# Diffusion trunk on one core: squares summed on DVE, second halves of five tiles, and two output tiles summed in one round

## Chip, cores and metric

The kernel runs on one core of a Trainium2 chip. The metric is device time in microseconds (us) of one execution. Engines: TensorE (PE), VectorE (DVE), ScalarE (ACT), GpSimd (POOL); SyncE (SP) issues the weight loads.

## The reference

One inference step of a two-layer trunk over 128 context tokens and 512 latent tokens (640 columns here), width 1024, all in fp32. Cut to what matters:

```python
for i in range(DEPTH):                       # 2 layers
    mod = (silu(cond) @ ada_w[i] + ada_b[i]) # 9 vectors of 1024: shifts, scales, gates
    h = modulate(rms_norm(x, norm_g[i, 0]), mod[:, 0], mod[:, 1])
    x = x + 0.5 * mod[:, 2] * swiglu(h, ffn_w_in[i, 0], ffn_w_out[i, 0])
    h = modulate(rms_norm(x, norm_g[i, 1]), mod[:, 3], mod[:, 4])
    o = even_mixer(h, ...) if i % 2 == 0 else odd_mixer(h, ...)   # both end in "@ w_out"
    x = x + mod[:, 5] * o
    h = modulate(rms_norm(x, norm_g[i, 2]), mod[:, 6], mod[:, 7])
    x = x + 0.5 * mod[:, 8] * swiglu(h, ffn_w_in[i, 1], ffn_w_out[i, 1])
y = rms_norm(x, final_norm)
```

The even mixer joins retention heads and spatial gating groups, the odd one is differential attention. Each of the six steps of the two layers is a phase here, 0 to 5; number 6 is the final norm.

## The kernel before

**Tiles.** Activations lie with channels on partitions and tokens along the free axis, in eight blocks of 128 channels. Tokens go in two halves, hf=0 and hf=1, of 320 columns each. An fp32 product is the sum of three matmuls (`mm3`, L717 to L719): high part by high part, low part of the activation by the high part of the weight, high part by the low part of the weight.

**Weights.** SP loads blocks of up to 1 MB into `raw` buffers, two at a time. A splitter makes pieces of them: the high part `whi` on ACT (L326), the remainder `wlo` on DVE (L327). There are five buffers for either part, and a piece is held until its last matmul is done. Loads of the adaLN weights `ada_w` go the same way; `ada` multiplies them with silu(cond) on TensorE (`adaps`, L469), copies the result out of PSUM (`adac`, on ACT at L477 or on DVE at L479), and sums the partial rows with L482.

**Projections back to x.** `out_proj` serves the second FFN matrix and the even mixer's output; each of its column groups gi (0 to 3) has two tiles j=0, 1. `op_step` sums a tile (gi, j, hf) in PSUM and `x_update` (L835, on DVE) adds it to x. The first two groups are done for both halves; then come the groups 2 and 3 for hf=0, then for hf=1. The last chunk of weights therefore stays until hf=1 has used it.

**Norm chains.** As soon as x of hf=0 is complete, `norm_chain` runs beside the tiles of hf=1. Squares are formed on ACT (L546) and summed on DVE (L550). TensorE sums over partitions (n10p for phase 1, L565; n20p, ... for the others). DVE works out one over the root in small steps (n10m, n10h, n10y, n10a, n10o, n10e, n10r) and builds diagonals n10d (L574), and TensorE spreads the result over all partitions (n10b, L577). H1t, H1h, H1l and the like (L629, L631, L636) are the next phase's normalised input in high and low parts. How many `mm3` steps pass in front of n10p and of n10b is set by the tables `NW` and `NB`. In these stretches TensorE's order is written by hand; that of DVE and ACT comes from a scheduler, in which chain and weight pieces share one queue.

**The head.** At the start eight blocks of x are squared on ACT (L1565). DVE adds the first `NQ` of them (L1571), and TensorE sums the rest together with DVE's sum (n0p, L1578), five columns of 128 tokens for each operand. While that goes on, `first_wide` runs the `ada` rounds of the first two modulation vectors (letters a and b of the table `SQ`) between the first matmuls `pf` of phase 0. Here the order of PE, DVE and ACT is that of the code.

**The odd mixer's output.** Its weight has two chunks of four heads, c=0 and c=1. The sums over c=0 (tiles m = 4 gp + 2 gi + j) are done during attention, in between the heads, and added to x; those of c=1 follow, hf=0 and then hf=1. The last head's transposes in attention are aot7a and aot7b (L1042).

## Time and profile before

| | us |
|---|---|
| median of 3 runs (lowest to highest) | 2433.4 (2432.97 to 2436.87) |
| profiled execution | 2431.29 |
| its span | 2429.5 |
| TensorE busy | 2389.4 (98%) |
| DVE busy | 1776.3 (73%) |
| ACT busy | 1063.9 (44%) |

The mean granted clock of TensorE is 0.994 of full. The chain that ended last is TensorE for 91% of the span, DVE for 4%, ACT and DMA for 2% each. An idle time of TensorE is therefore paid in full unless something else is late too; one of the other engines costs nothing by itself.

### The profile page before, as it was taken

How to read it: one execution, taken by the hardware profiler on the slowest of the kernel's cores; microseconds unless marked ns; L12 is line 12 of the kernel's file. 1: busy time of each engine (PE TensorE's matmuls, PEld its weight loads, DVE VectorE, ACT ScalarE, POOL GpSimd, SP SyncE). 2: the span in 40 equal slices, each digit the busy share in tenths (PEclk: the TensorE clock that was granted, in tenths of full speed). 3: DMA queues.
4: the chain of work that ended last, by engine and by line, in shares of the span. 5: the costliest groups of instructions: out<-in, count | busy, mean ns of one | idle time of the engine just before them, and what ended most of it. 6: DMA issues, size and time to landing. Idle time of an engine off the chain costs nothing.

```text
span 2429.5 us, 41107 instructions
## 1 busy us (share of the span) xinstructions
PE 2389.4 (98%) x16770; PEld 2338.1 (96%) x16770; DVE 1776.3 (73%) x3652; ACT 1063.9 (44%) x2013; POOL 54.0 (2%) x82
## 2 busy tenths in 40 slices
PE   8999999999999999999999999999999999999998
PEld 6999999999999999999999999999999989999997
DVE  5677767677968777676777776778789888574664
ACT  4425334333326344253543524446776645252442
POOL 0000000000000000000000000001011000000000
PEclk8999999999999999999999999999999999999999
DMA  6342413333242323333323242322111122222121
GB/s 238 148 147 88 156 70 113 129 136 123 90 157 87 139 90 122 129 113 139 122 79 141 98 153 104 122 106 76 44 43 59 55 105 86 72 87 87 70 105 44
DMA packets 44477, 259.33 MB, mean 107 GB/s; under 512 B 5888, under 2 KB 8576, under 8 KB 16768
## 3 DMA queue, kind: packets, MB, share of 16 engines
q1 hardware_dynamic: 41024, 252.37, 28.9%
q8 instruction: 131, 2.15, 0.3%
q0 software_dynamic: 1280, 2.62, 0.3%
q10 hardware_dynamic: 1984, 1.72, 0.2%
q14 instruction: 58, 0.48, 0.1%
HBM read 252.76 MB, written 3.93 MB: 106 GB/s over the span
## 4 chain that ended last, share of the span: by engine, by line
PE 91%; DVE 4%; ACT 2%; DMA 2%; issue 1%; POOL 0%; POOLq 0%; ACTq 0%; DVEq 0%
PE op L718 9%; PE op L717 9%; PE op L719 9%; PE pu L717 7%; PE pu L719 7%; PE pu L718 7%; PE pf L717 4%; PE pf L719 4%; PE pf L718 4%; PE pg L719 4%; PE pg L718 4%; PE pg L717 4%; PE oq L717 1%; PE atb L1422 1%; PE oq L718 1%; DVE wlo L327 1%
## 5 line engine op out<-in xcount | busy, mean ns | idle before, releaser
L327 DVE TENSOR_TENSOR wlo<-raw,whi 128x1024 fp32r<-128x1024 f32 (+1 forms) x482 | 531.6, 1119 | 277.5 <-ACT whi L326 275.6
L326 ACT ACTIVATE whi<-raw 128x1024 fp32r<-128x1024 f32 (+2 forms) x481 | 462.8, 977 | 601.1 <-PE op L718 146.9
L835 DVE SCALAR_TENSOR_TENSOR xs<-op,mod,xs 128x128 f32<-128x128 f32 (+2 forms) x312 | 124.1, 434 | 134.9 <-PE op L719 134.5
L546 ACT ACTIVATE nq<-xs 128x320 f32<-128x320 f32 x84 | 38.7, 467 | 116.1 <-DVE xs L835 114.6
L717 PE MATMUL oq<-H4h,whi 128*128 128x320 f32 x256 | 81.1, 318 | 0.2 <-ACT ov L1034 0.2
L719 PE MATMUL oq<-H4h,wlo 128*128 128x320 f32 x256 | 79.6, 311 | 0.0
L718 PE MATMUL oq<-H4l,whi 128*128 128x320 f32 x256 | 79.3, 310 | 0.0
L1371 DVE TENSOR_REDUCE amx<-as 128x1 f32<-128x320 f32 x144 | 61.5, 459 | 19.2 <-PE as L1367 18.8
L428 DVE CUSTOM_DVE_ANT_0 raw<-raw,sb 128x1024 f32<-128x1024 f32 x60 | 72.9, 1220 | 0.7
L1379 ACT ACTIVATE ap<-as,anm 128x320 f32<-128x320 f32 x128 | 66.1, 530 | 14.1 <-DVE anm L1374 13.7
L717 PE MATMUL pf<-H0p,whi 128*128 128x320 f32 x200 | 63.0, 317 | 0.0
L719 PE MATMUL pf<-H0p,wlo 128*128 128x320 f32 x200 | 62.3, 312 | 0.5 <-DVE wlo L327 0.5
L718 PE MATMUL pf<-H0p,whi 128*128 128x320 f32 x200 | 62.0, 311 | 0.0
L426 DVE SCALAR_TENSOR_TENSOR raw<-raw,sb 128x1024 f32<-128x1024 f32 x48 | 58.3, 1220 | 0.5
L924 ACT COPY p<-pg 128x320 f32<-128x320 f32 x75 | 32.0, 427 | 51.6 <-PE pg L719 51.6
L718 PE MATMUL pf<-H2p,whi 128*128 128x320 f32 x172 | 53.1, 309 | 0.0
L718 PE MATMUL pf<-H5p,whi 128*128 128x320 f32 x172 | 53.1, 309 | 0.0
L307 DVE TENSOR_TENSOR raw<-raw 128x512 f32<-128x512 f32 x75 | 51.7, 689 | 1.9
L718 PE MATMUL pf<-H3p,whi 128*128 128x320 f32 x172 | 53.1, 309 | 0.0
L717 PE MATMUL pf<-H2p,whi 128*128 128x320 f32 x172 | 53.0, 312 | 0.0
L717 PE MATMUL pf<-H5p,whi 128*128 128x320 f32 x172 | 53.0, 312 | 0.0
L717 PE MATMUL pf<-H3p,whi 128*128 128x320 f32 x172 | 53.0, 312 | 0.0
(2686 smaller groups left out, 8769.6 us busy)
## 6 DMA issues: line engine op xcount, KB each, us to landing
raw<-in_w_fin SPq DMA_DIRECT2D x88, 1024.0 KB, 4.8
raw<-in_ada_w SPq DMA_DIRECT2D x64, 1024.0 KB, 4.8
raw<-in_w_fout SPq DMA_DIRECT2D x32, 1024.0 KB, 4.7
raw<-in_w_fout SPq DMA_DIRECT2D x16, 768.0 KB, 4.1
raw<-in_w_oin SPq DMA_DIRECT2D x12, 1024.0 KB, 4.8
raw<-in_w_ein SPq DMA_DIRECT2D x10, 1024.0 KB, 4.8
raw<-in_ada_w SPq DMA_DIRECT2D x32, 256.0 KB, 6.5
raw<-in_w_eout SPq DMA_DIRECT2D x4, 1024.0 KB, 4.7
```

The costliest lines, as they stand in the source:

```text
L307: sub.tensor_tensor(out=a11, in0=a22, in1=a11, op=ALU.subtract)
L326: S.activation(out=hf, in_=t, func=AF.Copy)
L327: sub.tensor_tensor(out=lf, in0=t, in1=hf.bitcast(F32), op=ALU.subtract)
L426: V.scalar_tensor_tensor(out=o, in0=w, scalar=1.0, in1=sb[:, c * D:(c + 1) * D], op0=ALU.mult, op1=ALU.mult, accum_out=r)
L428: V.tensor_tensor_reduce(out=o, in0=w, in1=sb[:, c * D:(c + 1) * D], scale=1.0, scalar=0.0, op0=ALU.mult, op1=ALU.add, accum_out=r)
L546: S.activation(out=q[:, :n], in_=x[k][:, t0:t1], func=AF.Square)
L717: PE.matmul(o, wh, xh, start=start, stop=False, skip_group_check=more)
L718: PE.matmul(o, wh, xl, start=False, stop=False, skip_group_check=more)
L719: PE.matmul(o, wl, xh, start=False, stop=stop, skip_group_check=more)
L835: V.scalar_tensor_tensor(out=x[m][:, a:b], in0=ps[:, a - t0:b - t0], scalar=mod[:, l, gmod * KD + m, c:c + 1], in1=x[m][:, a:b], op0=ALU.m ...
L1371: V.tensor_reduce(out=mx[:, j, a:a + 1], in_=sps[j][a][:, 0:w], axis=AX.X, op=ALU.max, negate=True)
L1379: S.activation(out=pj[j][:, a * 320:a * 320 + w], in_=sps[j][a][:, 0:w], func=AF.Exp, bias=b, accum_out=(sm[:, j, a:a + 1] if full else s2 ...
```

## The change

Three parts. In the head `NQ` is 8, so DVE adds all squares, and the `ada` rounds of `first_wide` are given ACT for their copies. In `out_proj` the first part ends after three tiles of the first two groups (cut=3), and tile (1, 1) is done for hf=1 in the second half, which has five tiles in place of four; for the weight blocks in `jkeys` a piece now holds one output column block j over all k, so that half a block can be given back. The end (nxt=6) keeps its four tiles. In the odd mixer the c=0 sums of the two tiles gp=1, gi=1 of hf=1 are left out of attention; the weight piece is held, and in hf=1 those two tiles sum c=0 and c=1 in one PSUM round of 24 matmuls, ahead of the others. `NP5` and `NB5` place n50p and n50b.

```diff
-NQ = 5
+NQ = 8
 NB = (9, 9)
+NP5 = 11
+NB5 = 16
...
+    jkeys = {("fout", l, s, 2, g) for l, s in ((0, 0), (0, 1), (1, 0)) for g in (1, 2, 3)} | {("eout", g) for g in (1, 2, 3)}
...
+        elif key in jkeys:
+            nq, n = 1, wtab[key][1] * P
+            t = r[:, :2 * n].rearrange("p (k m x) -> p m k x", m=2, x=P)[:, h]
...
+            if order[self.j] in jkeys:
+                return [v[:, k * P:(k + 1) * P] for v in self.piece(m)]
...
-        yield NB[hf] if i < len(PHASES) else 9
+        yield (NB5 if (i, hf) == (5, 0) else NB[hf]) if i < len(PHASES) else 9
...
-                gs.append(ada(order[st["i"]]))
+                gs.append(ada(order[st["i"]], S))
...
     def out_proj(keys, acts, l, gmod, nxt, ks=None):
-        nw = len(keys) if nxt is None else 2
-        for gi in range(nw):
-            W = next_group(keys[gi])
+        end = nxt == len(PHASES)
+        js = [(gi, j) for gi in range(4) for j in range(2)]
+        cut = len(js) if nxt is None else 4 if end else 3
+        Ws = {}
+        for gi, j in js[:cut]:
+            if j == 0:
+                Ws[gi] = next_group(keys[gi])
...
+            for hf in range(2):
+                op_step(keys[gi], Ws[gi], gi, j, hf, acts, l, gmod, nxt, ks)
+                mid_ada()
+            if keys[gi] in jkeys:
+                Ws[gi].drop(j)
+            elif j == 1:
+                Ws[gi].done()
...
-            for gi in (2, 3):
-                if n_ == 0:
+            for gi, j in js[cut:]:
+                if gi not in Ws:
                     Ws[gi] = next_group(keys[gi])
...
-        def oo_step(c, gp, gi, j, hf, W, ps=None):
+        def oo_step(c, gp, gi, j, hf, W, ps=None, W0=None):
             m = 4 * gp + 2 * gi + j
-            for k in range(0 if ps is None else 3, 4):
+            if W0 is not None:
+                ps = psm(f"oo2{m}{hf}")
+                for k in range(4):
+                    mm3(ps, W0, j, 4 * gi + k, acts[k], hf, k == 0, False)
+            for k in range(3 if ps is not None and W0 is None else 0, 4):
...
-                    for hf in range(2):
+                    for hf in range(2 - gp * gi):
                         oo_step(0, gp, gi, j, hf, W)
-            W.done()
+            W.drop(*range(2 - gp))
+        held = W
...
-            for gp in range(2):
-                for gi in range(2):
-                    for j in range(2):
-                        oo_step(1, gp, gi, j, hf, Ws[gp], pss.get((gi, j)) if (hf, gp) == (0, 0) else None)
+            for gp, gi in ((0, 0), (0, 1), (1, 0), (1, 1)) if hf == 0 else ((1, 1), (0, 0), (0, 1), (1, 0)):
+                for j in range(2):
+                    oo_step(1, gp, gi, j, hf, Ws[gp], pss.get((gi, j)) if (hf, gp) == (0, 0) else None,
+                            held if hf * gp * gi else None)
```

How instructions move, at three places. First, ACT's order in the head from the last H0p of the first k row on. Before:

```order
L631 ACTIVATE H0p_148<-H0t_163,mod 128x320
L631 ACTIVATE H0p_149<-H0t_163,mod 128x192
L631 ACTIVATE H0p_149<-H0t_163,mod 128x128
L631 ACTIVATE H0p_150<-H0t_164,mod 128x320
L631 ACTIVATE H0p_151<-H0t_164,mod 128x192
L631 ACTIVATE H0p_151<-H0t_164,mod 128x128
L604 ACTIVATE H0t_164<-H0t_164,mod 128x512
```

After:

```order
L641 ACTIVATE H0p_148<-H0t_163,mod 128x320
L641 ACTIVATE H0p_149<-H0t_163,mod 128x192
L641 ACTIVATE H0p_149<-H0t_163,mod 128x128
L487 COPY adac_5_341<-adaps_5_332 128x256
L487 COPY adac_1_358<-adaps_1_349 128x256
L641 ACTIVATE H0p_150<-H0t_164,mod 128x320
L641 ACTIVATE H0p_151<-H0t_164,mod 128x192
```

The two copies, which stood on DVE, now stand between two H0p groups on ACT. Second, DVE at the boundary to phase 1, from the end of the small steps n10a to the diagonals n10d; `wlo` is a remainder of weights. Before:

```order
L509 SCALAR_TENSOR_TENSOR n10a_4774<-n10o,n10h 128x1 x3
L327 TENSOR_TENSOR wlo_1_4820<-raw_4705,whi_1_4819 128x1024
L520 SCALAR_TENSOR_TENSOR n10e<-n10a_4774 128x1 x3
L835 SCALAR_TENSOR_TENSOR xs<-op_0_2_2_11_4770,mod,xs 128x192
L835 SCALAR_TENSOR_TENSOR xs<-op_0_2_2_11_4770,mod,xs 128x128
L524 SCALAR_TENSOR_TENSOR n10r<-n10e,n10o 128x1
L327 TENSOR_TENSOR wlo_0_4838<-raw_4715,whi_0_4837 128x1024
L524 SCALAR_TENSOR_TENSOR n10r<-n10e,n10o 128x1 x2
L574 TENSOR_SCALAR n10d<-cst,n10r 128x128
L550 TENSOR_TENSOR nq_4418<-nq_4418,nq_4812 128x320
L574 TENSOR_SCALAR n10d<-cst,n10r 128x128
L574 TENSOR_SCALAR n10d<-cst,n10r 128x64
```

After:

```order
L335 TENSOR_TENSOR wlo_0_4729<-raw_4663,whi_0_4728 128x1024
L519 SCALAR_TENSOR_TENSOR n10a_4711<-n10y,n10h 128x1 x3
L560 TENSOR_TENSOR nq_4406<-nq_4406,nq_4721 128x320
L534 SCALAR_TENSOR_TENSOR n10o<-n10a_4711,n10y 128x1 x3
L519 SCALAR_TENSOR_TENSOR n10a_4732<-n10o,n10h 128x1 x3
L530 SCALAR_TENSOR_TENSOR n10e<-n10a_4732 128x1 x3
L534 SCALAR_TENSOR_TENSOR n10r<-n10e,n10o 128x1 x2
L845 SCALAR_TENSOR_TENSOR xs<-op_0_2_2_01_4724,mod,xs 128x192
L534 SCALAR_TENSOR_TENSOR n10r<-n10e,n10o 128x1
L584 TENSOR_SCALAR n10d<-cst,n10r 128x128 x2
L845 SCALAR_TENSOR_TENSOR xs<-op_0_2_2_01_4724,mod,xs 128x128
L584 TENSOR_SCALAR n10d<-cst,n10r 128x64
```

Two of the three remainders in the chain have moved behind n10d. Third, DVE at the boundary to phase 5, from the last diagonal n50d to the first low part of phase 5's input (H5p). Before:

```order
L574 TENSOR_SCALAR n50d<-cst,n50r 128x64
L550 TENSOR_TENSOR nq_21114<-nq_21114,nq_21183 128x320
L550 TENSOR_TENSOR nq_21114<-nq_21114,nq_21201 128x320
L550 TENSOR_TENSOR nq_21114<-nq_21114,nq_21225 128x320
L629 SCALAR_TENSOR_TENSOR H5t_21254<-xs,coefA,n50b 128x320
L629 SCALAR_TENSOR_TENSOR H5t_21255<-xs,coefA,n50b 128x320
L636 SCALAR_TENSOR_TENSOR H5p_21238<-H5t_21254,mod,H5p_21238 128x320
```

After:

```order
L584 TENSOR_SCALAR n50d<-cst,n50r 128x64
L845 SCALAR_TENSOR_TENSOR xs<-oo_21214,mod,xs 128x192
L845 SCALAR_TENSOR_TENSOR xs<-oo_21214,mod,xs 128x128
L560 TENSOR_TENSOR nq_21080<-nq_21080,nq_21165 128x320
L335 TENSOR_TENSOR wlo_1_21237<-raw_21051,whi_1_21236 128x1024
L639 SCALAR_TENSOR_TENSOR H5t_21260<-xs,coefA,n50b 128x320
L560 TENSOR_TENSOR nq_21080<-nq_21080,nq_21189 128x320
L845 SCALAR_TENSOR_TENSOR xs<-oo_21232,mod,xs 128x192
L845 SCALAR_TENSOR_TENSOR xs<-oo_21232,mod,xs 128x128
L639 SCALAR_TENSOR_TENSOR H5t_21261<-xs,coefA,n50b 128x320
L560 TENSOR_TENSOR nq_21080<-nq_21080,nq_21211 128x320
L646 SCALAR_TENSOR_TENSOR H5p_21244<-H5t_21260,mod,H5p_21244 128x320
```

A remainder and two updates of x (two instructions each) have come in between; three sums of squares stand there in both.

## Rows read from the trace of the kernel before

**Rows 1.** Waits of TensorE, whole span: line, releaser, total us, times, longest.

```profile
PE adaps L482 <- DVE adac L479: 3.3, 2, 2.2
...
PE n20b L577 <- DVE n20d L574: 2.0, 1, 2.0
```

**Rows 2.** Timeline of TensorE, head: start, us, instruction, count [idle before <-releaser].

```profile
16.05 5.77 PE L1578 MATMUL n0p<-cst,nq 128*128 128x1 f32 x40
21.75 1.93 PE L469 MATMUL adaps<-raw,sc 128*32 128x256 f32 x16
...
26.35 1.24 PE L1598 MATMUL n0b<-n0d,cst 128*128 128x320 f32 x4
...
28.41 1.07 PE L469 MATMUL adaps<-raw,sc 128*32 128x256 f32 x16
...
34.58 0.77 PE L482 MATMUL adaps<-cst,adac 128*128 128x128 f32 x4 [1.17 <-DVE adac L479]
...
37.03 1.93 PE L469 MATMUL adaps<-raw,sc 128*32 128x256 f32 x32
...
43.08 1.11 PE L482 MATMUL adaps<-cst,adac 128*128 128x128 f32 x4 [2.17 <-DVE adac L479]
```

**Rows 3.** Stretches: length, busy PE, PEld, DVE, ACT, POOL (count), PEclk, DMA share, GB/s.

```profile
15.60:19.20 3.60, 3.60 (x34) 3.60 (x33) 0.00 (x0) 0.00 (x0) 0.00 (x0) 0.97 0.92 342
19.20:21.80 2.60, 2.60 (x17) 2.58 (x20) 0.00 (x0) 0.00 (x0) 0.00 (x0) 0.50 1.01 335
...
43.00:46.20 3.20, 3.12 (x13) 3.08 (x14) 2.61 (x11) 1.04 (x3) 0.00 (x0) 0.50 0.89 289
484.00:490.00 6.00, 6.00 (x43) 6.00 (x42) 5.92 (x14) 3.25 (x6) 0.00 (x0) 1.00 0.31 94
```

**Rows 4.** Timeline of DVE and then of ACT, head, the same columns.

```profile
8.66 3.62 DVE L1571 TENSOR_TENSOR nq<-nq,nq 128x640 f32<-128x640 f32 x4 [7.19 <-ACT nq L1565]
...
23.95 1.07 DVE L1595 TENSOR_SCALAR n0d<-cst,n0r 128x128 f32<-128x128 f32 x5
...
23.75 0.37 ACT L477 COPY adac<-adaps 128x256 f32<-128x256 f32 x1 [8.73 <-PE adaps L469]
...
32.45 1.20 ACT L631 ACTIVATE H0p<-H0t,mod 128x320 fp32r<-128x320 f32 x3 [0.92 <-DVE H0t L629]
...
40.93 1.00 ACT L604 ACTIVATE H0t<-H0t,mod 128x512 f32<-128x512 f32 x2
```

**Rows 5.** SP's issue of the load, and its median us to landing, 25.9 to 26.5.

```profile
26.10 0.33 SPq L264 DMA_DIRECT2D raw<-in_ada_w  x1
...
raw<-in_ada_w SPq DMA_DIRECT2D x1, 256.0 KB, 5.3
```

**Rows 6.** Timelines of TensorE, ACT and DVE, boundary to phase 1, by start.

```profile
466.72 1.93 PE L469 MATMUL adaps<-raw,sc 128*32 128x256 f32 x32
...
472.72 1.06 ACT L326 ACTIVATE whi<-raw 128x1024 fp32r<-128x1024 f32 x1 [4.84 <-DMA raw<-in_w_ein]
...
473.81 1.23 DVE L327 TENSOR_TENSOR wlo<-raw,whi 128x1024 fp32r<-128x1024 f32 x1 [0.67 <-ACT whi L326]
...
474.96 0.16 DVE L499 TENSOR_SCALAR n10h<-n10m 128x3 f32<-128x3 f32 x1
...
478.48 1.22 DVE L327 TENSOR_TENSOR wlo<-raw,whi 128x1024 fp32r<-128x1024 f32 x1
...
480.35 0.45 DVE L574 TENSOR_SCALAR n10d<-cst,n10r 128x128 f32<-128x128 f32 x2
480.86 0.81 PE L577 MATMUL n10b<-n10d,cst 128*128 128x320 f32 x2 [2.10 <-DVE n10d L574]
```

**Rows 7.** Timeline of TensorE, end of attention and boundary to phase 5.

```profile
1948.17 0.60 PE L1042 MATMUL aot7a<-cst,aon 128*128 128x128 f32 x4
...
1957.60 1.93 PE L469 MATMUL adaps<-raw,sc 128*32 128x256 f32 x32
...
1972.65 0.78 PE L577 MATMUL n50b<-n50d,cst 128*128 128x320 f32 x2 [3.01 <-DVE n50d L574]
```

More of the change, by code (lines that the diff above doesn't have):

```diff
@@ L324, in split_piece @@
             hf, lf = hi[:, :n], lo[:, :n]
+            if key in jkeys:
+                hf, lf = (v.rearrange("p (k x) -> p k x", x=P) for v in (hf, lf))
         if early is None:
@@ L839, in out_proj @@
     def out_proj(keys, acts, l, gmod, nxt, ks=None):
-        nw = len(keys) if nxt is None else 2
-        for gi in range(nw):
-            W = next_group(keys[gi])
+        end = nxt == len(PHASES)
[5 more added lines that the diff above has]
+                Ws[gi] = next_group(keys[gi])
             if gi == 0 and keys[0][0] == "fout":
-                op_wide(keys[0], W, acts, l, gmod, nxt)
+                if j == 0:
+                    op_wide(keys[0], Ws[0], acts, l, gmod, nxt)
                 continue
-            for j in range(2):
-                for hf in range(2):
-                    op_step(keys[gi], W, gi, j, hf, acts, l, gmod, nxt, ks)
-                    mid_ada()
-            W.done()
-        if nw == len(keys):
+            for hf in range(2):
[5 more added lines that the diff above has]
+                Ws[gi].done()
+        if nxt is None:
             return
         la[0] = 2
-        Ws = {}
-        end = nxt == len(PHASES)
         for n_, hf in enumerate((1, 0) if end else (0, 1)):
@@ L859, in out_proj @@
                 pe_adas()
-            for gi in (2, 3):
-                if n_ == 0:
+            for gi, j in js[cut:]:
+                if gi not in Ws:
                     Ws[gi] = next_group(keys[gi])
-                for j in range(2):
-                    op_step(keys[gi], Ws[gi], gi, j, hf, acts, l, gmod, nxt, ks)
-                    mid_ada()
+                op_step(keys[gi], Ws[gi], gi, j, hf, acts, l, gmod, nxt, ks)
+                mid_ada()
                 if n_ == 1:
-                    Ws[gi].done()
+                    if keys[gi] in jkeys:
+                        Ws[gi].drop(j)
+                    elif j == 1:
+                        Ws[gi].done()
             chains[nxt, hf] = spawn(norm_chain(nxt, hf, NW[hf]))
@@ L1507, in oo_step @@
                     ps = psm(f"oo{c}{m}{hf}")
-                mm3(ps, W, j, 4 * gi + k, acts[4 * c + k], hf, k == 0, k == 3)
+                mm3(ps, W, j, 4 * gi + k, acts[4 * c + k], hf, k == 0 and W0 is None, k == 3)
             with tc.high_priority(HP):
@@ L1517, in odd_mixer @@
                 for j in range(2):
-                    for hf in range(2):
+                    for hf in range(2 - gp * gi):
                         oo_step(0, gp, gi, j, hf, W)
-            W.done()
+            W.drop(*range(2 - gp))
+        held = W
         while at in bgs:
@@ L1538, in odd_mixer @@
                 pe_adas()
-            for gp in range(2):
-                for gi in range(2):
-                    for j in range(2):
-                        oo_step(1, gp, gi, j, hf, Ws[gp], pss.get((gi, j)) if (hf, gp) == (0, 0) else None)
+            for gp, gi in ((0, 0), (0, 1), (1, 0), (1, 1)) if hf == 0 else ((1, 1), (0, 0), (0, 1), (1, 0)):
+                for j in range(2):
+                    oo_step(1, gp, gi, j, hf, Ws[gp], pss.get((gi, j)) if (hf, gp) == (0, 0) else None,
+                            held if hf * gp * gi else None)
                 if hf == 1:
-                    Ws[gp].done()
-            chains[nxt, hf] = spawn(norm_chain(nxt, hf, NW[hf]))
+                    Ws[gp].drop(gi)
+                    if gp * gi:
+                        held.drop(1)
+            chains[nxt, hf] = spawn(norm_chain(nxt, hf, (NP5, NW[1])[hf]))
     pump()
```

## The prediction

> **What bounds the kernel now.** TensorE is the engine that is busy nearly all the time, so what can be won is its idle time and the time in which it runs at half clock. I first read the waits of TensorE over the whole span [rows 1]. The change can touch six: two for DVE's `adac` copies in the head (3.3 together), and one each for n10b, n20b, n30b and n50b (2.1, 2.0, 2.0, 3.0; n30b's row repeats n20b's, the other two stand in the timelines). The wait of n60b lies at the end, which the diff leaves as it was. Then come the timelines of the head, of the boundary to phase 1 and of that to phase 5, because those waits lie there [rows 2, 4, 6, 7], the clock of the head by stretches [rows 3], and the landing of the head's loads [rows 5].
>
> **Part A, the head.** The sum of squares n0p now takes 40 matmuls in 5.77 us, 0.144 each, from 16.05 to 21.82 [rows 2]. After the change there are 10 (5 columns, two passes each): 1.44 us, end at 17.49, so 4.33 earlier. For that DVE must have added all eight squares by 16.05. Its four adds take 3.62 from 8.66 on, 0.905 each [rows 4]; seven end at 8.66 + 6.34 = 15.0. The three more adds are hidden by the weight loads that TensorE works on, with 1 us to spare; without that cover each would cost 0.9.
>
> From the end of n0p to n0b TensorE now takes 26.35 - 21.82 = 4.53 us, at half clock [rows 2, 3]. DVE's chain to the third n0d ends at 23.95 + 0.6 x 1.07 = 24.59, 2.77 after n0p [rows 4]. If the half clock stays, TensorE still sets n0b and the gain is 4.33. At full clock the 16 `adaps` take 1.07 in place of 1.93 [rows 2], and the warm-up matmuls and L482 behind them shrink in the same proportion: 4.53 becomes about 2.5. Then DVE sets n0b, at 17.49 + 2.8 = 20.3 in place of 26.35: 6.05. So the bounds are 4.33 and 6.05. Which one? The granted clock is full from 15.6, right before n0p, and is at half from 19.2, 3.2 us into these one-column matmuls [rows 3]. After the change they last 1.4, and wide `adaps` follow. I take 6.05, by the row in which 3 us of such matmuls had not yet lowered it.
>
> The Trainium skill (TensorE: Matmul & The Clock Gate, What's actually happening) says that the slow clock is the default and that activity releases it, and that the hardware's watch does not start with the kernel. By that the fall could come earlier in another execution, and n0b would move by 4.33 only, as in the first rival below. [...]
>
> Loads could bind next. The last piece of ada weights for the fourth round is issued at 26.10 and lands 5.3 later, at 31.4 [rows 5]. TensorE wants it 1 to 2 us behind 37.03 [rows 2], less 6.05 and 0.45 (below): 31.5 to 32.5. It just fits; a late one costs up to 0.5, and I put it at nothing.
>
> The `adac` copies go from DVE to ACT. At the first, TensorE waited until 34.58. ACT's H0p group before it ends at 33.65, and a copy takes 0.37 [rows 4], so with a hop L482 starts near 34.13: 0.45 won, not the whole 1.17, because the copies now queue behind ACT's H0p. At the second, TensorE waited 2.17, until 43.08. ACT's copies stand behind L604, which ends at 41.93 [rows 4], 0.45 earlier by the first step: 41.48 + 0.37 and a hop, 41.9. In all 1.18 is won, and 1.4 of wait remains (TensorE arrives at 40.91 - 0.45 = 40.46).
>
> After that wait of 2.17 the clock was at half for the 3.2 us from 43.0 to 46.2 [rows 3]; at full clock they are worth 1.6. The wait of 2.10 at n10b was followed by a full clock [rows 3]. With 1.4 left I take it that the clock holds. Of the 1.6 some 0.5 goes again: the first low piece of the next weights (1.2 on DVE) now comes behind ACT's two last copies, and TensorE meets it. Net 1.1, bounds 0 and 1.6. Head: 6.05 + 1.18 + 1.1 = **8.3**, bounds 4.3 and 8.8.
>
> **Part B, boundaries 1 to 4.** At boundary 1 TensorE finishes its tiles 12.04 us after `adaps` (480.86 - 2.10 - 466.72) and waits for n10d [rows 6]. In DVE's queue the chain n10 is interleaved with three weight remainders: one at 473.81, and two more, the second at 478.48, each 1.14 to the next start. From n10h at 474.96 to the end of n10d at 480.80 DVE has no gap: 5.84 us. After the change the order has a single remainder there, one sum of squares less (0.40), and n10h, n10y ahead of it (0.14): 5.84 - 2.28 - 0.40 - 0.14 = 3.02. From the end of the first remainder (8.24 after `adaps`; its load's landing does not move) that is 11.26, against 12.04 on TensorE, which still runs 24 matmuls ahead of n10p and 39 behind it. The wait goes entirely, with 0.8 to spare. What is late next? After n10b there are now 57 matmuls to the next phase in place of 33, with the same H operations and two remainders: no stall. Boundaries 2 and 3 repeat this; boundary 4 has no wait now. Splitting by output column moves no bytes and no instruction of ACT changes size. Five tiles instead of four means that pieces are wanted earlier; the tightest is boundary 2, where I find 1.5 us between a remainder's end and its use. B: 2.10 + 2.04 + 2.04 = **6.2**; from below 0 at each if the remainder in front of the chain comes 2.9 us later, so 0 to 6.2.
>
> **Part C, the odd mixer's output.** Matmuls stay the same in number; 24 go from the attention stage to the second half, and four x updates of DVE are saved. At boundary 5 TensorE arrived 1972.65 - 3.01 - 1957.60 = 12.04 after `adaps` and waited 3.01 [rows 7]. A matmul counts (12.04 - 1.93 - 0.7 for n50p) / 63 = 0.149. Now n50p comes 15 matmuls later and n50b has 60 between instead of 39: arrival 12.04 + 36 x 0.149 = 17.4. DVE's chain has to get past the remainder of the next weights whose high part ACT can write only when a held piece is freed, about 13.1 (the tile that holds it ends) + 1.1 + 1.2 = 15.4, then n50r, three n50d, two x updates and a sum, 1.7: 17.1. The 3.01 goes, by 0.3 only.
> Against that, two new waits. Only 21 matmuls now follow n50b, not 33, 3.1 us, while DVE has a remainder and two updates more ahead of the first H5p low part (near 22.0; TensorE is there at 20.9, both after `adaps`): 1.1. In the attention tail the 24 matmuls covered the last head's normalisation: 24 x 0.149 = 3.6 us less in front of aot7a, which now starts without a wait at 1948.17 [rows 7]. Its chain on ACT and DVE comes only 2.2 to 2.3 earlier (12 of the matmuls stood ahead of its start, of which 1.6 counts, and DVE has one update less): its last block at about 1945.9, where TensorE stands ready at 1944.6. That is 1.3 of wait. C: 3.01 - 1.1 - 1.3 = **+0.6**, bounds -2 (nothing won at n50b beyond 0.4) and +3.0.
>
> **Sum.** 8.3 + 6.2 + 0.6 = 15.1. The profiled execution took 2431.29 (its span 2429.5 and 1.8 around it), so it becomes 2416.2; the median of the runs is 2.1 above it: **2418.3**.
>
> **Rivals.** (1) The half clock stays in the head: n0b moves 4.33 only, and the second dip remains. Head 5.5, time 2433.4 - 12.3 = 2421.1. For it: the clock fell after a wait of 2.17 and during n0p; against it: both causes get shorter. (2) C turns into a loss: the two new waits are as above or longer and n50b keeps most of its own, -2.0: 2420.9. For it speaks the 0.3 of spare. (3) The change of order does not free the chain: the one remainder left in front of n10d still comes late, since it waits for a load (the high part waits for it until 472.72 [rows 6]); each wait keeps 1.7. B 1.1: 2423.4. Against it the 0.8 of spare, worked from rows without gaps. (1) and (3) together: 2426.2. All three: 2428.8, within 0.2% of now (0.2%, 4.9 us, is about what a measurement of this kernel can tell from no change). (4) On the other side: pieces held longer starve the splitter. It runs with five high and five low pieces; if tile (1,1)'s piece, kept to the second half, keeps the next load from being split, TensorE stands for a load and a split, 4.8 + 1.1 + 1.2 = 7.1 [rows 6], at a boundary. At all four of part B: 28.4, and B's gain gone: 2433.4 - 8.9 + 28.4 = 2452.9; from two boundaries on it is slower than now (2433.4 - 8.9 + 14.2 = 2438.7). Against it: the pieces are given back one by one, and I found 1.5 of spare at the tightest place.
>
> **How the numbers follow.** Forecast 0.40; (1) 0.27; (2) 0.11; (3) 0.10; two or three together 0.09; (4) 0.03. Of the 'together' cases most are still faster by over 4.9, but a loss in the loads of the head can come on top, so I give 0.09 to 'same' in all. The range: below, the forecast with C at +3 and the head at 8.8 (2415.4), a little more for the spread of the runs: 2414.5. Above, (1) with (3), 2426.2, and a little: 2427.0.
>
> **What would show it.** Head: n0p with 10 matmuls ending near 17.5; n0b near 20.3 (22.0 under (1)); a full clock up to the second L482 wait, and that wait near 1.4; `pf` of the first k rows some 6 us earlier. Boundaries: no row of n10b, n20b, n30b among the waits; if (3), rows of 1.7 each, released by n.0d. Boundary 5: no n50b row, instead `pf` waiting for H5p and aot7a waiting for aon, about 1.1 each. Under (4), `op` or `pf` waits for whi or wlo of several us. I would be wrong if DVE's adds ended behind 16.05, or if the second half of a boundary waited for weights.

## The result and the profile after

The changed kernel takes 2418.6 us (median of 4 runs, 2417.1 to 2421.6) against 2433.7 for the one before beside it: ratio 0.9935, interval 0.9922 to 0.9947. Five more runs of it beside other kernels gave 2417.65 (0.9931, 0.9918 to 0.9944). The forecast was 2418.3. Its profiled execution took 2418.53 (span 2416.4), that of before 2431.29, so from profile to profile 12.8 were won (13.1 by the spans), where the sum had said 15.1. That the median still agrees with the forecast has a reason of its own, which the experiments look for.

The waits of TensorE in the changed kernel, whole span (line, releaser, total us, times, longest), to lay beside [rows 1]:

```profile
PE n60b L587 <- DVE n60d L584: 2.7, 1, 2.7
PE adaps L492 <- ACT adac L487: 2.3, 2, 1.7
PE n41b L587 <- DVE n41d L584: 1.6, 1, 1.6
...
PE pf L728 <- DVE H5p L646: 0.8, 1, 0.8
PE n20b L587 <- DVE n20d L584: 0.7, 1, 0.7
...
PE n10b L587 <- DVE n10d L584: 0.4, 1, 0.4
...
PE aot7a L1059 <- DVE aon L1079: 0.2, 1, 0.2
```

n30b and n50b are gone, n10b and n20b have a rest, and n41b is new: boundary 4, at which the prediction put no wait. The head, first DVE's adds, then TensorE (the rows that answer to [rows 2, 4]):

```profile
8.55 6.41 DVE L1595 TENSOR_TENSOR nq<-nq,nq 128x640 f32<-128x640 f32 x7 [7.08 <-ACT nq L1589]
...
16.26 1.17 PE L1602 MATMUL n0p<-cst,nq 128*128 128x1 f32 x10
17.37 1.07 PE L479 MATMUL adaps<-raw,sc 128*32 128x256 f32 x16
...
20.30 1.34 PE L1622 MATMUL n0b<-n0d,cst 128*128 128x320 f32 x4
...
28.01 0.71 PE L492 MATMUL adaps<-cst,adac 128*128 128x128 f32 x4 [0.56 <-ACT adac L487]
...
36.00 0.71 PE L492 MATMUL adaps<-cst,adac 128*128 128x128 f32 x4 [1.71 <-ACT adac L487]
```

The adds end at 14.96, n0b starts at 20.30, and the clock (last but two of the numbers of a stretch) has no fall in n0p and none behind the second wait, where [rows 3] had 0.50 twice:

```profile
11.50:15.00 3.50, 3.50 (x18) 1.30 (x19) 3.14 (x4) 1.25 (x3) 0.00 (x0) 0.50 1.06 384
...
16.00:20.00 4.00, 4.00 (x43) 3.40 (x42) 2.19 (x14) 1.43 (x2) 0.00 (x0) 0.97 1.00 391
...
36.00:40.00 4.00, 4.00 (x36) 3.16 (x37) 3.76 (x14) 1.42 (x4) 0.00 (x0) 1.00 0.85 314
```

How far each kernel is ahead of the profiled execution of before at the same product, in us; the last columns belong to the experiments below (head: part A alone; halves: B alone; round24: C alone; no_head: B and C; lamp: all, with two loads on another queue):

| at | whole change | again | head | halves | round24 | no_head | lamp |
|---|---|---|---|---|---|---|---|
| n11b, before 497.57 | 10.1 | 10.6 | 4.5 | 1.2 | -0.4 | 0.7 | 9.8 |
| n21b, 742.95 | 11.4 | 12.9 | 2.9 | 3.5 | -0.5 | 3.0 | 12.1 |
| n31b, 1190.54 | 14.4 | 15.3 | 3.4 | 6.5 | -0.7 | 5.6 | 14.8 |
| n41b, 1634.44 | 12.3 | 13.3 | 2.8 | 5.2 | -0.9 | 4.2 | 16.1 |
| n51b, 1989.66 | 13.1 | 14.1 | 1.4 | 2.7 | -0.1 | 5.0 | 16.4 |

The whole change has 8.2 at the first `pf` behind the head (58.02 before, 49.79 now). Then boundary 1 gives 1.9, boundary 2 1.3, boundary 3 3.0, the stage behind it, in which small waits of `pu` change places, takes 0.5, boundary 4 takes 1.6, and boundary 5 gives 0.8.

### The profile page after: what moved, and what is told of

Same layout as the page of the kernel before. It is cut to its first block, busy times and chain, and to the rows that moved or that the text cites. A ratio compares the mean times of both kernels' runs of the same rounds, so it can differ in the third digit from the quotient of the medians.

```text
span 2416.4 us, 41049 instructions
## 1 busy us (share of the span) xinstructions
PE 2383.4 (99%) x16740; PEld 2331.6 (96%) x16740; DVE 1774.4 (73%) x3645; ACT 1064.1 (44%) x2019; POOL 53.0 (2%) x82
## 3 DMA queue, kind: packets, MB, share of 16 engines
q8 instruction: 131, 2.15, 0.4%
## 4 chain that ended last, share of the span: by engine, by line
PE 90%; DVE 4%; ACT 2%; DMA 2%; issue 1%; POOL 0%; POOLq 0%; SPq 0%; ACTq 0%; DVEq 0%
PE op L727 9%; PE op L728 9%; PE op L729 9%; PE pu L727 7%; PE pu L729 7%; PE pu L728 7%; PE pf L727 4%; PE pf L728 4%; PE pf L729 4%; PE pg L729 4%; PE pg L727 3%; PE pg L728 3%; DMA raw<-in_w_fin 1%; PE atb L1439 1%; PE adaps L479 1%; PE oq L727 1%
## 5 line engine op out<-in xcount | busy, mean ns | idle before, releaser
L845 DVE SCALAR_TENSOR_TENSOR xs<-op,mod,xs 128x320 f32<-128x320 f32 (+2 forms) x312 | 124.6, 435 | 125.0 <-PE op L729 124.7
L1396 ACT ACTIVATE ap<-as,anm 128x320 f32<-128x320 f32 x128 | 66.1, 530 | 14.1 <-DVE anm L1391 13.9
```

Of the source, the lines that this page charges most:

```text
L845: V.scalar_tensor_tensor(out=x[m][:, a:b], in0=ps[:, a - t0:b - t0], scalar=mod[:, l, gmod * KD + m, c:c + 1], in1=x[m][:, a:b], op0=ALU.m ...
L1396: S.activation(out=pj[j][:, a * 320:a * 320 + w], in_=sps[j][a][:, 0:w], func=AF.Exp, bias=b, accum_out=(sm[:, j, a:a + 1] if full else s2 ...
```

## The experiments

Times, each beside the kernel before on the same chip (2433.8, 2434.5 and 2434.3 in the three series):

| kernel | median (range), runs | ratio to before (95%) |
|---|---|---|
| head | 2428.9 (2424.8 to 2431.6), 11 | 0.9977 (0.9969 to 0.9986) |
| halves | 2427.4 (2424.4 to 2428.6), 7 | 0.9971 (0.9960 to 0.9982) |
| round24 | 2433.1 (2430.2 to 2439.4), 12 | 1.0001 (0.9993 to 1.0009) |
| lamp | 2415.0 (2414.5 to 2416.6), 4 | 0.9925 (0.9912 to 0.9938) |
| fill | 2432.7 (2430.9 to 2438.3), 11 | 0.9993 (0.9982 to 1.0004) |
| head_fill | 2427.1 (2422.0 to 2436.8), 12 | 0.9970 (0.9959 to 0.9980) |
| whole | 2417.7 (2416.5 to 2421.3), 5 | 0.9931 (0.9918 to 0.9944) |
| no_head | 2426.5 (2423.5 to 2429.6), 5 | 0.9964 (0.9950 to 0.9977) |
| lamp_b | 2415.7 (2414.7 to 2417.1), 5 | 0.9920 (0.9907 to 0.9934) |
| lamp_warm | 2414.7 (2413.8 to 2416.0), 4 | 0.9917 (0.9903 to 0.9930) |

### Part A alone (head)

```diff
-NQ = 5
+NQ = 8
...
-                gs.append(ada(order[st["i"]]))
+                gs.append(ada(order[st["i"]], S))
```

> This kernel carries part A alone (eight squares summed by DVE, `adac` copies on ACT); parts B and C are as before. Theory: A is worth what the anchors of the two traces show, 8.2 us by the first pf, and nothing of it is lost or multiplied later, since behind the head the order is that of before: 8.2 faster, with n0p in 10 matmuls, n0b near 20.3, a full clock from 16 on, and the waits of n10b, n20b, n30b and n50b as before (2.0 to 3.0 each). Rival: part of the 13.1 that the whole change gained belongs to the three parts only together (loads that arrive earlier against the chains); then the gain at the end differs from that at the first pf by over 1 us. If the half clock is a matter of chance from one execution to the next, n0b is near 22.0 here and the gain 5.5.

Measured: 5.6 us (0.0023 of 2433.8; 3.4 to 7.5), not 8.2. At n10p the trace is 8.35 ahead; at the end 1.2 are left. Boundary 1 shows both ways in which it went, in the timelines of ACT and TensorE and in the stretch behind:

```profile
465.59 1.06 ACT L326 ACTIVATE whi<-raw 128x1024 fp32r<-128x1024 f32 x1 [6.06 <-DMA raw<-in_w_ein]
...
473.73 1.44 PE L577 MATMUL n10b<-n10d,cst 128*128 128x320 f32 x2 [3.32 <-DVE n10d L574]
```

The stretch there (its clock is the last number but two):

```profile
474.00:479.00 5.00, 5.00 (x18) 4.61 (x19) 2.40 (x6) 1.49 (x3) 0.00 (x0) 0.50 0.13 56
```

ACT waited 6.06 for the load, 1.22 more than in [rows 6], and n10b waits 3.32 instead of 2.10, the same 1.22 more. Behind that wait TensorE runs at half clock (0.50, 1.2 GHz): from n10b to n11p it takes 12.91, before 10.32, so the fall costs 2.6. The same happened at n20b (wait 2.17, cost 1.5) and n50b (3.11, cost 1.2), and not at n30b (2.23). In the profiled execution of before none of the four waits (2.04 to 3.01) was followed by a fall. So the rival held, by a mechanism that neither theory had: **a wait of a boundary is sometimes followed by half clock**, in one execution and not in another.

### Part B alone (halves)

```diff
+    jkeys = {("fout", l, s, 2, g) for l, s in ((0, 0), (0, 1), (1, 0)) for g in (1, 2, 3)} | {("eout", g) for g in (1, 2, 3)}
...
-        nw = len(keys) if nxt is None else 2
...
+        cut = len(js) if nxt is None else 4 if end else 3
```

> This kernel carries part B alone (boundaries 1 to 4 cut behind three tiles, weights split by output column); the head and the odd mixer are as before. The prediction put it at 6.2 (2.10 + 2.04 + 2.04, boundary 4 nothing). The trace of the changed kernel says 1.85 + 1.30 + 3.0 at boundaries 1 to 3 and a loss of 1.6 at boundary 4 (n41b waits for n41d, because lamp's DMA stands behind a buffer-blocked weight load in SP's queue): 4.6 faster. Rival to the loss: n41b's wait comes from the other parts (an earlier head, part C); then it is absent here, and the gain is near 6.2. Rival to the 0.4 and 0.7 that n10b and n20b still wait: they are the landing of the first of two loads, which was 5.9 and 6.2 us in that execution against 4.8 and 4.7 before; if the landing varies freely, these waits are gone here, if it belongs to the new order, they stand again.

Measured: 7.1 us (4.4 to 9.7), which holds both 4.6 and 6.2. In the profiled execution, the slowest of the seven runs, neither n10b, n20b nor n30b waits. n41b does, as in the whole change, so its wait belongs to part B:

```profile
1629.25 0.78 PE L587 MATMUL n41b<-n41d,cst 128*128 128x320 f32 x2 [1.56 <-DVE n41d L584]
```

From n11b on the table shows 2.3, 2.9 and -1.3 at boundaries 2, 3 and 4. The 1.2 at n11b are 2.4 at boundary 1 less 1.1 that this execution lost in the head. At boundary 5 it fell to half clock behind n50b's wait of 3.02 and lost 2.4, part of the 2.5 between n41b and n51b.

### Part C alone (round24)

```diff
-                    for hf in range(2):
+                    for hf in range(2 - gp * gi):
                         oo_step(0, gp, gi, j, hf, W)
-            W.done()
+            W.drop(*range(2 - gp))
+        held = W
```

> This kernel carries part C alone (two tiles of the odd mixer's output summed in one round in the second token half); head and boundaries 1 to 4 are as before. The prediction put it at 0.6: the 3.01 of n50b gone, 1.1 of wait at pf for H5p, 1.3 at aot7a for aon. The trace of the changed kernel says 0.8 faster, with pf 0.8 and aot7a 0.2, and some 1.2 that no named wait holds. Rival: aot7a's wait was short only since part B or the head shifted the loads against the attention tail; then it is 1.3 here and the whole is at or below 0.

Measured: no difference that can be told (1.0001, from 1.7 faster to 2.2 slower); its trace gains 0.9 from n41b to n51b. The 3.01 of n50b is gone; pf waits 0.79 for H5p. aot7a looks free at first, but it isn't:

```profile
1946.18 1.11 PE L1052 MATMUL aot7a<-cst,aon 128*128 128x128 f32 x4 [0.17 <-DVE aon L1072]
```

Its four matmuls take 1.11 where [rows 7] has 0.60, since they wait for aon block by block. From the last matmul of oo6 in front of it to the first of oo4 behind it 1.62 pass (1945.70 to 1947.32), before 0.61 (1948.02 to 1948.63): it costs 1.0, of which the row calls 0.17 a wait.

### The two small loads on another queue (lamp, lamp_b)

```diff
-        nc.sync.dma_start(out=lpt, in_=lamp)
+        nc.gpsimd.dma_start(out=lpt, in_=lamp)
...
-        nc.sync.dma_start(out=sl_, in_=subln)
+        nc.gpsimd.dma_start(out=sl_, in_=subln)
```

This and the next explain boundary 4. SP's queue there in the timeline of before (n40b is at 1617.56):

```profile
1616.06 0.33 SPq L273 DMA_DIRECT2D raw<-in_w_oin  x1
1616.48 0.86 SPq L1067 DMA_DIRECT2D rot<-in_consts  x2
1617.39 0.71 SPq L1281 DMA_DIRECT2D lpt<-in_lamp  x1
...
1623.69 0.33 SPq L273 DMA_DIRECT2D raw<-in_w_oin  x1
```

In the changed kernel (n40b at 1600.15):

```profile
1600.62 8.18 SPq L276 DMA_DIRECT2D raw<-in_w_oin  x2
1608.85 0.91 SPq L1084 DMA_DIRECT2D rot<-in_consts  x2
1609.79 0.70 SPq L1298 DMA_DIRECT2D lpt<-in_lamp  x1
```

What follows from it in the changed kernel's timelines of DVE and TensorE:

```profile
1615.02 0.29 DVE L1306 TENSOR_TENSOR lpr<-lpt 128x128 f32<-128x128 f32 x1 [3.10 <-DMA lpt<-in_lamp]
...
1622.10 0.78 PE L587 MATMUL n41b<-n41d,cst 128*128 128x320 f32 x2 [1.56 <-DVE n41d L584]
```

In these rows SP issues one after the other. Before, the second load of w_oin comes behind the small ones; in the changed kernel both stand in front of them, and the second waits for a buffer that DVE gives back with a remainder that ends at 1608.4: the pair takes 8.18 to issue. lpt goes out 9.6 behind n40b instead of at it, DVE stands 3.10 at `lpr`, and the chain to n41d is queued behind.

> The changed kernel, with the two small loads of the odd mixer (lpt and subln) on POOL's queue in place of SP's, where they stand behind a weight load that waits for a buffer. Theory: boundary 4 lost its 1.6 through that place in SP's queue; lpt then lands before DVE wants it, the wait of lpr (3.1 on DVE) and that of n41b (1.6 on TensorE) are gone, and the kernel is 1.6 faster than the changed one, near 2417 as a median. Rival: n41b's chain is late on DVE whatever lpt does, as it has a remainder more ahead of it; then lpr waits no more, n41b still waits over 1 us, and the time is that of the changed kernel.

Measured: 2415.0. `lpt` is issued at 1579.97, `lpr` finds it there, and n41b doesn't wait (timelines of POOL, DVE and TensorE):

```profile
1579.97 0.54 POOL L1298 DMA_DIRECT2D lpt<-in_lamp  x1
...
1609.88 0.28 DVE L1306 TENSOR_TENSOR lpr<-lpt 128x128 f32<-128x128 f32 x1
...
1618.32 0.70 PE L587 MATMUL n41b<-n41d,cst 128*128 128x320 f32 x2
```

The theory held, the rival fell. The Trainium skill (Trainium Kernel Development and Optimization, Key Constraints) says that issuing DMAs from several engines only saves the sequencer's issue time. Here it also takes a small load from behind one that waits for a buffer. On TensorE the 1.56 of wait is gone, and from n40b to n41b 20.12 us pass in all three profiles with the loads on POOL's queue, where it is 21.9 to 22.0 in the four that have part B and the loads on SP's: 1.8.

> The changed kernel with the two small loads of the odd mixer (lpt, subln) on POOL's queue, once more, to stand beside the whole change on the same chip. By the wait that it took away it is 1.6 faster than the whole (n41b 1.56 in the changed kernel, no wait here); 3.6 between the two medians so far would be 2 too much for that and would have to be the head's clock in the runs of the one or the other. So: 1.6 faster if both see the head's clock equally often, up to 3.6 if that was not chance.

Measured: 2415.7, 2.0 below the whole change beside it. Over both series nine runs lie between 2414.5 and 2417.1 (median 2415.6), nine of the whole change between 2416.5 and 2421.6 (2418.5). That is 2.9, of which boundary 4 explains 1.8. The rest isn't settled, but in the profiles it isn't the head's clock: n0b is at 20.30 and 19.41 in the whole change, at 20.01 and 20.45 in lamp and lamp_b. The stage ahead of boundary 4 differs, from n31b to n40p 417.6 and 417.5 against 416.05 and 416.03: in the whole change ACT waited 1.9 and 2.0 for a load of w_fin (at 1348), in the others 0.6 and 0.5, and TensorE waits 0.8 and 0.9 for a1010s in the first two alone. This lies before the moved loads are used, so it doesn't come from `lpr`'s wait; whether the runs without a profile share it isn't known.

### Fillers in the waits (fill, head_fill)

```diff
+        for _ in range(FILL if (i, hf) in ((1, 0), (2, 0), (3, 0), (5, 0)) else 0):
+            PE.matmul(bc[:, 0:P], ones, ones, start=True, stop=True)
         PE.matmul(bc[:, :n], ones, dg[:, :n], start=True, stop=True)
```

FILL is 6; fill is on the kernel before, head_fill on part A alone.

> The kernel before, with six matmuls of constants (some 1.6 us, into n10b's, n20b's, n30b's and n50b's own bank, overwritten by the real product) ahead of each of the four products that wait: the chains on DVE are as late as before, TensorE is only kept busy in most of the wait. Theory, formed from the profiles of the four kernels so far: behind a wait of 2 to 3 us the clock falls to half in some executions and not in others, which costs 1.3 to 2.6 each time. Then here the clock is 1.00 at all four boundaries, the rows of the four waits shrink to 0.4 to 1.5, the median is near 2431.3 (the profiled execution of before, which had no fall at the boundaries) in place of 2433.8, and the runs lie closer together than 2430 to 2437. Rival: the scatter of before has nothing to do with the clock; then median and scatter are those of before, or 0.5 worse for the matmuls that come behind n.0d.

Measured: 0.9993, 1.8 faster by the medians, and the interval holds 1. At boundary 1, TensorE's timeline and the stretch around it:

```profile
476.70 1.50 PE L579 MATMUL n10b<-cst 128*128 128x128 f32 x12
478.99 0.81 PE L580 MATMUL n10b<-n10d,cst 128*128 128x320 f32 x2 [0.79 <-DVE n10d L575]
```

The stretch there (its clock is the last number but two):

```profile
476.00:482.00 6.00, 5.21 (x37) 4.86 (x37) 4.79 (x16) 1.58 (x4) 0.00 (x0) 1.00 0.50 178
```

All four stretches have a clock of 1.00, and the waits are 0.8 to 1.5. So that half of the theory is seen: the clock is held where TensorE is kept busy. That it makes the median faster is not shown, since the interval holds 1. The scatter isn't gone: seven runs at 2430.9 to 2433.0, four at 2437.5 to 2438.3. It has to do with the clock all the same, against the rival: the mean granted clock of the four is 0.992 or 0.993, that of the seven 0.994 to 0.996. Where the clock fell in the four is open, as no profile shows one of them.

> Part A alone, with the same filling matmuls at the four boundaries. Part A alone measured 5.6 us (3.4 to 7.5), while its trace had won 8.3 by n10p; the rest went in half-clock stretches behind the waits of n10b (2.6), n20b (1.5) and n50b (1.3), and in a load that landed 1.2 later at boundary 1. Theory: with the clock held, part A keeps 8.2 less the 1.2 of n10b: 7.0 under the filled kernel before, near 2424.3. Rival: the gain of the head is lost to the order of loads and remainders on DVE; then the waits grow beyond the filling, and the difference stays at 5 to 5.6.

Measured: 0.9970, 7.3 faster than before (4.9 to 10.0). Against fill, with which the theory and the rival compare, it is 5.6 by the medians and by the ratios: the rival's 5 to 5.6, though the scatter of both kernels doesn't rule out 7.0. Its profiled execution, the slowest of the twelve runs, shows why it can be less. At boundary 1 the first load was late (ACT waited 6.34), the wait grew beyond the fillers to 2.26, and the clock fell in spite of them:

```profile
477.42 0.81 PE L580 MATMUL n10b<-n10d,cst 128*128 128x320 f32 x2 [2.26 <-DVE n10d L575]
```

The stretch there (its clock is the last number but two):

```profile
476.00:482.00 6.00, 4.58 (x19) 4.43 (x20) 3.79 (x13) 1.49 (x3) 0.00 (x0) 0.72 0.37 153
```

A second price is paid later. On ACT, then TensorE:

```profile
1470.41 1.57 ACT L327 ACTIVATE whi<-raw 128x1024 fp32r<-128x1024 f32 x2 [4.41 <-DMA raw<-in_w_fin]
...
1472.36 0.64 PE L720 MATMUL pu<-T30ah,whi 128*128 128x320 f32 x1 [3.30 <-ACT a1014s L930]
```

A load issued at 1462.54 was there 7.9 later, ACT stood at `whi` with the copy that TensorE wanted behind it, and half clock followed to 1478: 4.7 lost from n31b to n40p in a stage that the edits don't touch.

### The two edits of the head apart (nq8, copies)

nq8 has only `NQ = 8`, copies only the `S` of the second line of head's diff. Each has one run, the profiled one (2429.3 and 2431.5), so the times say little and the timelines are read.

> The kernel before with all eight squares of the head summed on DVE, the `adac` copies left on DVE. By the prediction's term: n0p has 10 matmuls, n0b moves by 6.05 to near 20.3 at full clock; the second wait for adac stays at 2.2 and the clock falls again behind it (1.6). So the first pf of the main stream is about 6 earlier and not 8.2. Rival: with n0p short the copies on DVE are met earlier, and the waits for adac grow by as much as n0b gains (n0b 20.3, but the first wait 1.2 or more longer).

Measured, TensorE's timeline of the head:

```profile
16.42 2.13 PE L1578 MATMUL n0p<-cst,nq 128*128 128x1 f32 x10
...
23.50 1.54 PE L1598 MATMUL n0b<-n0d,cst 128*128 128x320 f32 x4
```

The stretch there (its clock is the last number but two):

```profile
12.00:16.00 4.00, 4.00 (x23) 2.02 (x19) 2.73 (x4) 0.84 (x2) 0.00 (x0) 0.50 1.10 375
16.00:20.00 4.00, 4.00 (x29) 3.06 (x28) 1.21 (x8) 0.00 (x0) 0.00 (x0) 0.50 0.95 358
20.00:24.00 4.00, 4.00 (x19) 3.49 (x16) 2.36 (x14) 1.33 (x2) 0.00 (x0) 0.50 1.05 402
```

Neither theory: n0b moves by 2.85 only. The clock had not risen when n0p began, and stayed at half until 24.1 (the 24.9 in two of the expectations below is too late); n0p takes 2.13 in place of 1.17, and what stands between it and n0b nearly twice its time too. The first `pf` of the main stream is 2.4 earlier, not 6. head_fill's head is the same (n0b 23.46, half clock until 24.2). In the other kernels with ten matmuls (the whole change twice, head, lamp, lamp_b) the clock rose before or at the start of n0p, and n0b is at 19.4 to 20.5: five of seven. The Trainium skill (TensorE: Matmul & The Clock Gate, What's actually happening) says that the watch on TensorE's activity runs on by itself and doesn't start with the kernel, so that the release comes earlier or later from run to run. These rows agree that it varies, and by more than the half us to either side that the page gives there: the clock rose at 14.6 to 16.3 us in five of the seven profiles, at 24.1 and 24.2 in two.

> The kernel before with the `adac` copies on ACT, n0p with its 40 matmuls as before. By the prediction's terms: the first wait ends 0.45 earlier, the second is near 1.4 to 1.7 in place of 2.17, and the clock holds behind it: 1.18 + 1.1 by the first pf of the main stream, with the fall inside n0p as before. Rival: the fall behind the second wait belongs to something else (the fall of 19.2, or chance); then it stands again at 43, and 1.2 or less is won.

Measured: the theory. The second wait is 1.47, and the stretch that had 0.50 in [rows 3] runs at full clock; n10p is 2.6 earlier, where 1.18 + 1.1 was expected.

```profile
41.80 0.70 PE L482 MATMUL adaps<-cst,adac 128*128 128x128 f32 x4 [1.47 <-ACT adac L477]
```

The stretch there (its clock is the last number but two):

```profile
43.00:46.20 3.20, 3.20 (x32) 2.42 (x31) 3.13 (x11) 1.44 (x4) 0.00 (x0) 1.00 0.82 312
```

Later it fell behind n10b (2.15, cost 1.5) and n20b (2.20, cost 1.6), and ended level with the profiled execution of before.

### The whole without part A, and the whole again (no_head, whole)

no_head is the changed kernel with the two edits of head's diff undone.

> Parts B and C without part A: the head is that of before. Alone, A measured 5.6, B 7.1 and C within 2 of nothing, 12.7 in sum, the whole change 15.1. Theory: A's gain is lost in part behind the waits of the boundaries, where the clock falls in some executions, and B and C take these waits away; with B and C in place A is worth its 8.2 less a chance of 3 in the head, so this kernel is 7 to 8 slower than the whole, near 2426. Rival: the parts simply add, and 12.7 against 15.1 is scatter; then it is 5.6 slower, near 2424.

Measured: 2426.5, 8.8 above the whole beside it (8.0 by the ratios). Part A alone was worth 5.6. The intervals overlap, so the times don't prove that the parts help each other; the traces show a path by which they can, head's three falls behind waits that B and C remove. This execution also had the latest first load at boundary 1 of all, on ACT and then TensorE:

```profile
471.36 1.06 ACT L334 ACTIVATE whi<-raw 128x1024 fp32r<-128x1024 f32 x1 [6.75 <-DMA raw<-in_w_ein]
...
476.68 0.81 PE L587 MATMUL n10b<-n10d,cst 128*128 128x320 f32 x2 [1.19 <-DVE n10d L584]
```

> The changed kernel once more, for a second profile of it and for times beside the next three. Where the head's clock rises before n0p (16.1 in its first profile, 15.2 and 14.8 in those of part A alone and of the kernel with lpt on POOL's queue), n0b is at 19.8 to 20.3; where it has not risen by then, as in two of the five profiles with ten matmuls in n0p, it stays at half to 24.9 and n0b is at 23.5. So the runs should spread over some 3 us, 2417 to 2422, about a median near 2419; n41b waits 1.5 again, and n10b and n20b 0 to 0.8 according to the landing of their loads. Rival: the first profile was typical and the head's clock no matter of chance; then the runs spread by 1 us.

Measured: 2417.65, four runs at 2416.5 to 2418.7 and one at 2421.3, as in the first four (2421.6 the highest). Its profile has the clock up before n0p and n0b at 19.41. n41b waits 1.57, n10b 0.7, n20b not at all. The two highest of all nine runs, 2421.3 and 2421.6, have a mean granted clock of 0.995, the seven others 0.996 or 0.997. So these two ran longer at half clock; that it was in the head would fit the 3 us, but no profile caught one in this kernel.

### More warm-up in the first wait (lamp_warm)

```diff
-WU = (12, 4, 4, 1, 4)
+WU = (28, 4, 4, 1, 4)
```

> The same with 28 warm-up matmuls in place of 12 at the very start, in the 5 us in which TensorE waits for the first ada weights (6.3 to 11.5). Theory: the half clock from 11.5 to 15 or to 24.9 is that of an engine that stood idle in front of it; kept busy until some 11 us, it starts at full clock: `adaps` takes 1.5 in place of 3.0, n0p then waits for DVE's adds (end near 15.0), n0b is near 19.0 in every execution. That is 1.0 to 1.3 faster than the kernel without it where its clock rose in time, 4.5 where it did not: near 2413 as a median, and the runs closer together. Rival: the clock in the head goes by its own time and not by what the engine did; then the half clock stands at 11.5 to 15 as before, and nothing is won.

Measured: 2414.7, 1.0 below lamp_b; the intervals overlap, so it can't be told from it. The mechanism is as the theory had it: 1.00 in the stretch that has 0.50 above, and all four runs have a mean granted clock of 0.998, where those of lamp and lamp_b have 0.996 or 0.997.

```profile
12.00:16.00 4.00, 3.91 (x32) 2.24 (x28) 2.79 (x4) 0.91 (x2) 0.00 (x0) 1.00 1.04 358
```

TensorE, at the end of the head's chain:

```profile
19.77 1.24 PE L1622 MATMUL n0b<-n0d,cst 128*128 128x320 f32 x4
```

n0b is at 19.77, not 19.0: `adaps` still takes 2.55 for want of its loads, and n0p starts at 15.16, right behind DVE's adds. Against a head whose clock rises in time that is little; against one where it doesn't it would be 3.7 (23.50 - 19.77). It beats both kernels of this case: 0.9917 of before, and all its runs lie below all nine of the changed kernel.

## Why the prediction was right, and where it was not

**Part A, 8.3.** Measured 8.2 at the first `pf`, here and in part A alone. n0b at 20.30 is 6.05 earlier, as written: n0p took 1.17 instead of 1.44 but began 0.2 later. The two waits gave 1.03 (1.18 was expected; the second is 1.71, not 1.4), and what follows the second one gave 1.15 (1.1). The fall that is gone was worth 1.44 (1.6), and the low piece of the next weights is met late as the prediction said, by 0.3 (0.5); TensorE's row has no wait, its matmul starts when DVE's remainder ends (DVE, TensorE):

```profile
43.85 1.22 DVE L335 TENSOR_TENSOR wlo<-raw,whi 128x1024 fp32r<-128x1024 f32 x1 [1.94 <-ACT whi L334]
...
45.13 0.42 PE L729 MATMUL pf<-H0p,wlo 128*128 128x320 f32 x1
```

What the step did not have right is the nature of its alternative. It weighed a fall after 1.4 us of narrow matmuls. What happens instead, in two of seven profiles, is that the clock has not yet risen, and n0b is then at 23.5, not at the 22.0 of rival (1), because n0p is slow too (2.13).

**Part B, 6.2.** Measured 1.9 + 1.3 + 3.0 - 1.6 = 4.6 in the first profile. The chain on DVE is as computed. Boundary 1 in the changed kernel, ACT, DVE, TensorE:

```profile
461.93 1.06 ACT L334 ACTIVATE whi<-raw 128x1024 fp32r<-128x1024 f32 x1 [5.94 <-DMA raw<-in_w_ein]
...
463.02 1.22 DVE L335 TENSOR_TENSOR wlo<-raw,whi 128x1024 fp32r<-128x1024 f32 x1 [1.49 <-ACT whi L334]
...
466.96 0.24 DVE L584 TENSOR_SCALAR n10d<-cst,n10r 128x64 f32<-128x64 f32 x1
...
467.26 0.81 PE L587 MATMUL n10b<-n10d,cst 128*128 128x320 f32 x2 [0.38 <-DVE n10d L584]
```

Only one remainder is ahead of n10d, and what is left of the wait is the load's. ACT's wait for the first load at the boundary, and the wait of the product, over the profiles:

| order | kernel and boundary | ACT waits for the load | product waits | difference |
|---|---|---|---|---|
| before | before, 1 | 4.84 | 2.10 | 2.74 |
| before | head, 1 | 6.06 | 3.32 | 2.74 |
| part B | whole change, 1 | 5.94 | 0.38 | 5.56 |
| part B | whole again, 1 | 6.26 | 0.71 | 5.55 |
| part B | no_head, 1 | 6.75 | 1.19 | 5.56 |
| part B | whole change, 2 | 6.27 | 0.73 | 5.54 |
| part B | lamp_b, 2 | 6.99 | 1.44 | 5.55 |
| part B | halves, 1 | 5.27 | 0 | |
| part B | lamp_warm, 1 | 4.83 | 0 | |

A us of late load is a us of wait, and part B gives 2.81 more room; the prediction's chain was shorter by 5.84 - 3.02 = 2.82. Its spare of 0.8 was right too (5.55 - 4.84 = 0.71). The step that failed is "its load's landing does not move": at boundaries 1 and 2 ACT waits 4.8 to 7.0 for the first load. Whether that is chance alone is open at boundary 1: the four kernels with five squares on DVE and the old order there (before, round24, fill, copies) have 4.84 to 4.90, nine of the ten other profiles 5.27 to 6.75, so that work which comes earlier may meet a later load. At boundary 2 the same kernel shows both. Rival (3), which named the load, thus comes true in part and not as a fixed 1.7.

**Boundary 4.** The prediction says "boundary 4 has no wait now", and puts it at nothing. That was the wrong step. With part B the second load of w_oin stands ahead of the small loads in SP's queue and waits for a buffer. The prediction followed DVE and TensorE there and not SP. It cost 1.6, and lamp gives it back.

**Part C, 0.6.** Measured 0.8. The 3.01 went, H5p cost 0.8 (1.1 was expected), aot7a 1.0 (1.3), and atb 0.1 more than before; some 0.3 of the difference isn't found. Each new wait is where it was put and smaller by 0.3; in the waits of TensorE alone aot7a would have been missed. The spare of 0.3 at n50b is as thin as written: in lamp's profile n50b waits 0.64.

**The sum and the median.** The sum gave 2416.2 for a profiled execution; it took 2418.5, 2.3 more. Lost were boundary 4 (1.6), the two late loads (0.4 and 0.7), the stage ahead of boundary 4 (0.5) and 0.3 outside the span; boundary 3 gave 1.0 more than its 2.04. Against that, the prediction carried over the 2.1 by which the median of before lay above its profile, and that did not carry over: the profile of the changed kernel lies at its median. Falls of the clock explain the 2.1, though no single run proves it. Of the 21 waits of 2.0 to 3.3 at boundaries 1, 2, 3 and 5 in all these profiles 7 were followed by half clock, at 1.2 to 2.6 each, 1.8 in the mean. Before has four such waits, so as an estimate 4 x 7 / 21 x 1.8 = 2.4 in an average execution; its profiled one had none. The runs that have no profile agree, since each has its mean granted clock on record: of the 57 runs of the kernel before in the three series, 16 at 0.994 or 0.995 took 2430.5 to 2434.9, 27 at 0.993 took 2431.5 to 2436.3, and 14 at 0.990 to 0.992 took 2436.3 to 2441.9; the profiled execution is at 0.994. Between the head and the last norm no fall follows a wait of 1.0 to 1.7 in these profiles, and the changed kernel has no longer one there. So **two errors of 2 us met**: the trace won less than the sum, and the median won the falls besides. That the forecast came within 0.3 us of the median is luck; the parts are right to 0.3 us in A and C, and off by 1.6 in B. Of the rivals, (1) comes true in some executions, by another mechanism, (3) in part, and (4) left no trace: beyond the 0.3 in the head, no product waited for `whi` or `wlo` longer than before.

Open are the 0.3 to 1.0 that boundary 3 gave beyond its wait of 2.04 in every kernel with part B, the place of the falls in the upper runs of fill, and in how many executions of the changed kernel the head's clock comes late. The two pieces of part B, the five tiles and the weights split by output column, were not run apart.

## What to carry to other kernels

A wait is worth more than its length where half clock can follow it, and one profile shows only one throw: before a profile's waits are summed, compare its time and its mean granted clock with those of the other runs, and ask which of the waits fell. A load that a chain depends on has a range of landing times, so give the spare of the chain against the latest one seen. When an edit moves the instruction that frees a buffer, follow the queue of the loads too: a small load behind one that waits for a buffer is as late as that buffer.
